# A Conformer stage in a two-layer trunk: block taps loaded by DMA, a fourth channel tile convolved on VectorE with its sum in PSUM, 24 low halves of weights made on GpSimd

## The chip, the cores and the metric

The kernel runs on one core of one Trainium2 chip. A core has a matrix engine (TensorE, "PE" in the profile; its weight loads are "PEld"), a vector engine (VectorE, "DVE"), a scalar engine (ScalarE, "ACT"), a general engine (GpSimd, "POOL"), and a queue that issues transfers between the chip's memory and the core (SyncE, "SP"). Each engine works through its own list of instructions in order and waits on semaphores for the others. SBUF is the core's working memory of 128 partitions, and PSUM a smaller one of eight banks, each 128 partitions x 512 float32, in which TensorE leaves its results.

The metric is the device time of one execution in microseconds. Lower is better.

## The reference

The program is a decoder trunk of two layers over 512 positions of 1024 channels, float32 throughout. Layer 0 mixes positions by a gated DeltaNet, layer 1 by a Conformer convolution; each layer then attends to a memory of 256 rows and applies an MLP of width 4096. The change lies in layer 1's Conformer:

```python
def conformer_conv(h, w_pw1, b_pw1, w_dw, b_dw, ln_g, ln_b, w_pw2, b_pw2):
    u = h @ w_pw1 + b_pw1
    u = u[..., :D_MODEL] * jax.nn.sigmoid(u[..., D_MODEL:])
    c = causal_depthwise_conv(u, w_dw) + b_dw
    c = jax.nn.silu(layer_norm(c, ln_g, ln_b))
    return c @ w_pw2 + b_pw2
...
for layer in range(DEPTH):
    if layer % 2 == 0:
        h = h + gated_deltanet(rms_norm(h, dn_norm[j]), ...)
    else:
        h = h + conformer_conv(rms_norm(h, cv_norm[j]), ...)
    h = h + memory_cross_attention(rms_norm(h, xa_norm[layer]), rms_norm(mem, ...), ...)
    h = h + sq_relu_mlp(rms_norm(h, mlp_norm[layer]), ...)
return rms_norm(h, final_norm)
```

The depthwise convolution is causal and has 31 taps per channel. `w_pw1` maps 1024 channels to 2 x 1024 (a value and a gate), `w_pw2` 1024 to 1024.

## The kernel before

**Products.** Every float32 product is made of three matrix products of halves. A weight block of 128 x 1024 comes in as `raw` (line 203); ACT casts it to the high half `wh` (line 214), and DVE subtracts that from `raw` to give the low half `wl` (line 215; the profile shows line 72, the helper `tt`). The activations are split likewise. `mm3` then adds high x high, high x low and low x high (lines 230 to 232). A block with its two halves is called a unit here; it gives 24 matmuls. Units are taken in a fixed order, the list `order`. `wnext` loads raw blocks some units ahead (`NRAW` = 3 buffers) and splits them ahead (`NW` = 3 buffers for each half). A raw buffer can be loaded again when both halves of the block that it held are made.

**The Conformer stage.** Activations are held as channels on partitions and positions along them, in eight channel tiles of 128 x 512; position t stands at column (t mod 4, t div 4), so that four phases lie beside each other. The stage goes through `CONV_SEQ`: 16 pw1 units (two for each channel tile m: value and gate), then 16 units of layer 1's K and V, which belong to the cross-attention that follows and depend on the memory alone. They keep TensorE supplied while the convolution is finished.

When both pw1 units of a tile are done, `pw_ev` scales them by the norm (`sg` and `pa`, DVE reading PSUM), applies the sigmoid on ACT, and multiplies. A tile is then convolved in one of two ways:

- Tiles 0 to `NDVE` - 1 = 2 go by taps on VectorE (`dve_conv`). The product is written into a padded copy `x7` with three more shifted phases. The first tap is an ACT multiplication into `ca`; 30 `scalar_tensor_tensor` instructions on DVE (line 75, `ca<-x,prm,ca`) then each add one tap: x times a scalar plus the sum, 128 x 512. They are kept in a list `todo`, from which `taps_dve` takes some after each unit, at `TAP_RATE` per microsecond. `turn` transposes the sum by four TensorE transposes (`cvT`, line 1041) and adds it into Y.
- Tiles 3 to 7 go by block form on TensorE (`conv`). Sixteen transfers copy `glu` into `xg` (line 1014), with 32 channels x 4 phases on the partitions. For each group j of 32 channels, nine matmuls (lines 1057 and 1060) multiply `xg` with block tap matrices, so 36 matmuls for a tile. The block taps, nine tiles of 128 x 512 for each channel tile, are made by `taps`: POOL multiplies a broadcast identity with a broadcast row of `prm`.

Both ways end in Y, which holds positions on partitions and channels along them and starts as the bias `b_dw`; for each quarter of the positions, DVE adds into `cy` and takes statistics `bn`. When all eight tiles are there, `ln` normalizes Y, and `ln_out` transposes it back (`lnT`), applies scale, bias and silu on ACT and splits the result for pw2.

**What sets the order.** `CONV_AFTER` says after which unit of `CONV_SEQ` each of these is issued: ("t", m) block taps, ("c", m, ...) groups of a block convolution, ("d", m) the transposes of a DVE tile, ("l", 0) the LayerNorm, ("o", m) `lnT`. The block taps of tile 3 are made in layer 0's MLP. A list scheduler then orders the instructions of each engine by its own estimate of when they are due; it may put instructions of one engine in another order than the program's. SP's queue carries the weights and the `xg` copies in such an order too.

**Memory.** `slot` hands out SBUF buffers of 128 x 512 from a pool of `NSLOT` = 66, `psum` banks from a pool of eight. A request waits until the oldest holder is done.

Of the kernel before, what the change touches and what calls it, by code (L numbers as in the profile page):

```python
# [8 lines left out]
F32 = mybir.dt.float32  # L9
F32R = mybir.dt.float32r  # L10
AF = mybir.ActivationFunctionType
ALU = mybir.AluOpType
AX = mybir.AxisListType

P = 128
NT = 512
NDVE = 3
KT = 8
EPS = 1e-6
LN_EPS = 1e-5  # L20
# [3 lines left out]
OFF = {n: 8 * i for i, n in enumerate(_VECS)}  # L24
_o = 8 * len(_VECS)
# [1 line left out]
_o += 16  # L27
OFF["w_conv"] = _o
_o += 24 * 4
OFF["w_dw"] = _o  # L30
_o += 8 * 144
OFF["w_tap"] = _o
_o += NDVE * 31
OFF["out_norm"] = _o
# [3 lines left out]


@with_exitstack  # L40
def tile_trunk(ctx, tc, xT, memT, prm_d, adt_d, bdw_d, fin_d, w_ab, w_kq, w_v, w_z, w_dno, w_pw1, w_pw2,
               w_q, w_k, w_vv, w_o, w_up, w_dn, yT):
    nc = tc.nc
    pe, act, dve, pool = nc.tensor, nc.scalar, nc.vector, nc.gpsimd
# [14 lines left out]
    def slot(dt=F32, s="u", shape=(P, NT)):  # L59
        return up.tile(list(shape), dt, tag="u", name=nm(s))  # L60
# [7 lines left out]
    def const(shape, s, dt=F32):  # L68
        return cp.tile(list(shape), dt, tag=s, name=s)

    def tt(e, o, a, b, op):
        e.tensor_tensor(out=o, in0=a, in1=b, op=op)  # L72

    def stt(o, a, s, b, op0, op1):
        dve.scalar_tensor_tensor(out=o, in0=a, scalar=s, in1=b, op0=op0, op1=op1)  # L75
# [7 lines left out]
    def c4(t):  # L83
        return t.rearrange("p (c i) -> p c i", c=4)
# [4 lines left out]
    def over_c(t, n=4):  # L89
        return t.unsqueeze(1).to_broadcast([P, n, t.shape[1]])  # L90


    prm = const([P, NPRM], "prm")
# [9 lines left out]
        return r  # L103

    nc.sync.dma_start(out=prm[:, 0:NVEC], in_=prm_d[:, 0:NVEC])
    wab = const([P, P], "wab")
    nc.sync.dma_start(out=wab, in_=w_ab)
    raw0 = wp.tile([P, 1024], F32, tag="raw", name="raw0", bufs=NRAW)
    nc.sync.dma_start(out=raw0, in_=w_kq[0][:, 0:1024])
# [4 lines left out]
    ident = const([P, P], "ident")  # L114
# [21 lines left out]
    headx = const([P, 32], "headx")  # L136
    dve.tensor_reduce(out=headx, in_=ident.rearrange("p (x c) -> p x c", c=4), op=ALU.add, axis=AX.X)
    dve.tensor_reduce(out=headm, in_=headx.rearrange("p (a h) -> p h a", h=8), op=ALU.add, axis=AX.X)
    ident4 = const([P, 32], "ident4")
    eps_rms = const([P, 1], "eps_rms")  # L140
    pool.memset(eps_rms, EPS)
    eps_ln = const([P, 1], "eps_ln")
# [3 lines left out]
    order, srcs = [], {}  # L146
# [26 lines left out]
    for kind, gq in DN_ORDER:  # L173
        for i in range(2):
            j = gq * 2 + i
# [30 lines left out]
    def wsplit():  # L206
        u = ws["split"]
        ws["split"] += 1
        while ws["load"] <= u:
            wload()  # L210
        raw = ws["raw"].pop(u)
        h = wp.tile([P, 1024], F32R, tag="wh", name=nm("wh"), bufs=NW)
        lo = wp.tile([P, 1024], F32R, tag="wl", name=nm("wl"), bufs=NW)
        act.copy(h, raw)  # L214
        tt(dve, lo, raw, h.bitcast(F32), ALU.subtract)
        ws["hl"][u] = (h, lo)

    def wnext(key, hf):
# [544 lines left out]
    def mem_gain(layer, half):  # L763
        gn = f"xa_mem{layer}"
        if half == 0:
            mem["xs"] = []
        for j in (2 * half, 2 * half + 1):
            mh = slot(F32R, "mh")
            ml = slot(F32R, "ml")
            for i in range(2):  # L770
                ks = slice(i * 256, (i + 1) * 256)
                src = mem["n"][j][:, ks]
                g = pc(gn, 2 * j + i)
                act.activation(mh[:, ks], src, AF.Copy, scale=g)
                stt(ml[:, ks], src, g, mh[:, ks].bitcast(F32), ALU.mult, ALU.subtract)
                mem["xs"].append((mh[:, ks], ml[:, ks]))

    KV = {}
# [191 lines left out]

    def taps(m):

        w = OFF["w_dw"] + 144 * m
        TAPS[m] = []
        for i in range(9):
            t = slot(s="tap")
            tt(pool, t.rearrange("p (a c) -> p a c", c=32), over_c(ident4, 16),
               prm[:, w + 16 * i:w + 16 * i + 16].unsqueeze(2).to_broadcast([P, 16, 32]), ALU.mult)
            TAPS[m].append(t)

    def conformer(norm, hres, nxt):
        xs = norm.xs
        st, xg = {}, {}
# [35 lines left out]

        def dve_conv(m, x7):  # L1020

            a = acc[m] = slot(s="ca")

            def tap(d):
                w, u, e = pc("w_tap", m * 31 + 30 - d), d // 4, d % 4
                src = x7[:, 3 - e:7 - e, 8 - u:136 - u]
                if d == 0:
                    act.activation(c4(a), src, AF.Copy, scale=w)
                else:
                    stt(c4(a), src, w, c4(a), ALU.mult, ALU.add)  # L1030

            return [lambda d=d: tap(d) for d in range(31)]

# [91 lines left out]

    nc.sync.dma_start(out=prm[:, NVEC:NPRM], in_=prm_d[:, NVEC:NPRM])
    nc.sync.dma_start(out=adt, in_=adt_d.partition_broadcast(P))
    for b in range(4):
        bs = slice(32 * b, 32 * b + 32)
        pool.tensor_copy(ident4[bs, :], ident[bs, bs])  # L1130
    abp = const([P, 2 * P], "abp", F32R)
    ab3 = abp.rearrange("p (k x) -> p k x", k=KT)
    act.copy(ab3[:, :, 0:16], wab.rearrange("p (k x) -> p k x", k=KT))
    tt(dve, ab3[:, :, 16:32], wab.rearrange("p (k x) -> p k x", k=KT), ab3[:, :, 0:16].bitcast(F32), ALU.subtract)
# [129 lines left out]
    n2 = Norm("mlp_norm0")  # L1264
    h = xattn(0, n1, h, n2)
    n3 = Norm("cv_norm", deng=pool)
    h = mlp(0, n2, h, n3, lambda: (mem_gain(1, 0), mem_gain(1, 1), taps(3)))
    n4 = Norm("xa_norm1")
    h = conformer(n3, h, n4)
    n5 = Norm("mlp_norm1")  # L1270
# [12 lines left out]
    def finish(hid, cur):  # L1283
# [3 lines left out]
        for c, g in LAST:  # L1287
# [14 lines left out]
            if g == 0:  # L1302
# [14 lines left out]
    mlp(1, n5, h, None, None, finish, load)  # L1317


NSLOT = 66  # L1320
NCV = 6
NRAW = 3
PRE = ((2, 4), (2, 6))
# [17 lines left out]
REC = (39, 68)  # L1341
MEM = 53
MLP_ORDER = [("up", 0), ("up", 1), ("dn", 0), ("up", 2), ("dn", 1), ("up", 3), ("dn", 2), ("dn", 3)]
TAP_RATE = 0.75
CONV_SEQ = [("p", i) for i in range(16)] + [("k", i) for i in range(16)]
CONV_AFTER = [(3, ("t", 4)), (9, ("c", 3, 0, 1)), (11, ("c", 3, 2, 3)), (11, ("t", 5)), (12, ("c", 4, 0, 1)),
              (13, ("c", 4, 2, 3)), (13, ("t", 6)), (14, ("c", 5, 0, 1, 2, 3)), (14, ("t", 7)), (15, ("d", 0)),
              (16, ("c", 6, 0, 1, 2, 3)), (17, ("d", 1)), (18, ("c", 7, 0, 1, 2, 3)), (20, ("d", 2)), (20, ("l", 0))]
CONV_AFTER += [(24 + _m, ("o", _m)) for _m in range(8)]


# [18 lines left out]

def _taps(np, w):

    wt = w.T.reshape(8, 4, 32, 31)
    e = np.zeros((4, 32, 8, 4, 9, 4), w.dtype)
    for s in range(4):
        for u in range(9):
            for r in range(4):
                d = r - s + 4 * u
                if 0 <= d <= 30:
                    e[s, :, :, :, u, r] = wt[:, :, :, 30 - d].transpose(2, 0, 1)  # L1380
    e = e.reshape(128, 8, 4, 9, 4)
    return np.concatenate([e[:, :, :, 0:8].reshape(128, 8, 128), e[:, :, :, 8].reshape(128, 8, 16)],
                          axis=2).reshape(128, 1152)


def _layout(np, i):
    i = {k: np.asarray(v) for k, v in i.items()}
    f = np.ascontiguousarray

    def vec(v):  # L1390
        return v.reshape(-1, 128).T

    r = {}
    r["xT"] = f(i["x"][0].T)
    r["memT"] = f(i["mem"][0].T.reshape(4, 2, 128, 256).transpose(0, 2, 1, 3).reshape(4, 128, 512))
    vecs = [i["dn_norm"][0], i["cv_norm"][0], i["xa_norm"][0], i["xa_norm"][1], i["xa_mem_norm"][0],
            i["xa_mem_norm"][1], i["mlp_norm"][0], i["mlp_norm"][1], i["cv_ln_g"][0],
            i["cv_ln_b"][0], i["cv_b_pw2"][0], i["cv_b_pw1"][0]]
    cols = [vec(v) for v in vecs]
    cols.append(i["dn_w_conv"][0].T.reshape(24, 128, 4).transpose(1, 0, 2).reshape(128, 96))  # L1400
    cols.append(_taps(np, i["cv_w_dw"][0]))
    cols.append(i["cv_w_dw"][0].T.reshape(8, 128, 31)[:NDVE].transpose(1, 0, 2).reshape(128, NDVE * 31))
    cols.append(i["dn_out_norm"][0].reshape(128, 1))
    r["prm"] = f(np.concatenate(cols, axis=1))
    r["adt"] = f(np.concatenate([i["dn_a_log"][0], i["dn_dt_bias"][0]]))
    r["bdw"] = f(i["cv_b_dw"][0])
    r["fin"] = f(i["final_norm"])
    w = i["dn_w_in"][0]
    r["w_ab"] = f(w[:, 4096:].reshape(8, 128, 16).transpose(1, 0, 2).reshape(128, 128))
    r["w_kq"] = _pack_a(np, w[:, :2048], [8, 9, 10, 11, 0, 1, 2, 3, 12, 13, 14, 15, 4, 5, 6, 7])  # L1410
    r["w_v"] = _pack_a(np, w[:, 2048:3072])
    r["w_z"] = _pack_b(np, w[:, 3072:4096])
    r["w_dno"] = _pack_a(np, i["dn_w_out"][0])
    r["w_pw1"] = _pack_a(np, i["cv_w_pw1"][0], [m for h in range(8) for m in (h, 8 + h)])
    r["w_pw2"] = _pack_a(np, i["cv_w_pw2"][0])
    r["w_q"] = np.stack([_pack_a(np, i["xa_w_q"][j]) for j in range(2)])
    r["w_k"] = np.stack([_pack_a(np, i["xa_w_kv"][j][:, :1024]) for j in range(2)])
    r["w_vv"] = np.stack([_pack_b(np, i["xa_w_kv"][j][:, 1024:]) for j in range(2)])
    r["w_o"] = np.stack([_pack_a(np, i["xa_w_o"][j]) for j in range(2)])
    r["w_up"] = np.stack([_pack_a(np, i["mlp_w_up"][j]) for j in range(2)])  # L1420
    r["w_dn"] = np.stack([np.concatenate([(_pack_b if (j, g) == (1, 3) else _pack_a)(
        np, i["mlp_w_down"][j][g * 1024:(g + 1) * 1024]) for g in range(4)]) for j in range(2)])
    return r
# [17 lines left out]
```

## Time and profile before

| | |
|---|---|
| median of 3 runs | 1583.6 us |
| lowest and highest | 1582.46 and 1584.26 us |
| the profiled execution, whole | 1584.79 us |
| its span in the profile | 1583.1 us |
| TensorE clock granted in it (1 is full) | 0.984 |

The span runs from the first to the last instruction that the profiler recorded; the whole time of the same execution is 1.7 us longer. The page cuts the span in 40 slices of about 39.6 us and gives the busy share of each engine in tenths:

```profile
PE   8997997999999999999999999999999999999998
DVE  6785787576555444343445599974545443443441
ACT  6655574645444433231424321164434432322332
POOL 1225224402111100000021316102012000000000
PEclk9998998799999999999999999999999999999999
```

The Conformer stage lies at about 880 to 1096 us, slices 23 to 28 counted from 1. A row of a timeline has a start, a length, the engine, the line, the operation, the tiles (output, then inputs) and a count where several stand together; idle time before it and what ended it follow in brackets. A row of groups has the count, then busy time in all and the mean of one in nanoseconds, then idle time of the engine before them. A row of waits has the time in all, how often, and the longest. A row of windows has the stretch and its length, then for each engine the busy time and the count, the clock granted, the share of time in which the transfer engines were busy, and the rate in GB/s. Instructions of one engine overlap by some 0.08 us, so lengths add up to a little more than the time that passes.

### The profile page before, as it was taken

The numbers are of one execution on the slowest core, as the hardware profiler recorded it, in microseconds if no ns is written. First come the engines' busy times: TensorE is split into PE (matmuls) and PEld (weight loads), VectorE is DVE, ScalarE is ACT, GpSimd is POOL, SyncE is SP. The second block draws the span as 40 slices with busy tenths as digits, with TensorE's granted clock in tenths as the row PEclk, the third lists the DMA queues.
The fourth block names the chain that finished last, engine by engine and source line by source line (L and its number), as shares of the span: only waits on it lengthen the run. The fifth ranks groups of instructions, "written<-read, shape, count | busy, mean of one in ns | idle before, by whom it ended". The sixth has DMA issues, their size and how long they took to land.

```text
span 1583.1 us, 19556 instructions
## 1 busy us (share of the span) xinstructions
PE 1539.9 (97%) x7690; PEld 1300.1 (82%) x7690; DVE 897.3 (57%) x1290; ACT 652.5 (41%) x997; POOL 239.5 (15%) x287
## 2 busy tenths in 40 slices
PE   8997997999999999999999999999999999999998
PEld 6886885898888888888888889888888888888886
DVE  6785787576555444343445599974545443443441
ACT  6655574645444433231424321164434432322332
POOL 1225224402111100000021316102012000000000
PEclk9998998799999999999999999999999999999999
DMA  5221112153211233223223422253212232223231
GB/s 180 67 80 54 59 49 94 54 173 119 91 61 64 93 98 102 94 94 101 98 94 95 146 79 92 77 164 103 80 41 94 93 104 96 94 96 104 94 107 53
DMA packets 46699, 147.57 MB, mean 93 GB/s; under 512 B 6288, under 2 KB 8976, under 8 KB 46608
## 3 DMA queue, kind: packets, MB, share of 16 engines
q1 hardware_dynamic: 46608, 146.33, 28.4%
q8 instruction: 60, 0.98, 0.3%
q14 instruction: 31, 0.25, 0.0%
HBM read 142.90 MB, written 2.10 MB: 92 GB/s over the span
## 4 chain that ended last, share of the span: by engine, by line
PE 79%; DVE 11%; ACT 4%; issue 2%; POOL 2%; SPq 1%; DMA 1%; DVEq 0%; POOLq 0%; ACTq 0%
PE up L230 7%; PE up L232 7%; PE up L231 7%; PE dn L232 6%; PE dn L231 6%; PE dn L230 6%; DVE ca L75 3%; PE q L230 2%; PE xo L231 2%; DVE wl L72 2%; PE q L231 2%; PE q L232 2%; PE xo L232 2%; PE xo L230 2%; PE pw L230 2%
## 5 line engine op out<-in xcount | busy, mean ns | idle before, releaser
L214 ACT CAST wh<-raw 128x1024 fp32r<-128x1024 f32 x248 | 260.2, 1051 | 699.6 <-PE dn L231 190.4
L72 DVE TENSOR_TENSOR wl<-raw,wh 128x1024 fp32r<-128x1024 f32 x248 | 310.3, 1252 | 128.6 <-ACT wh L214 122.5
L230 PE MATMUL up<-xh,wh 128*128 128x512 f32 x512 | 200.2, 391 | 0.0
L232 PE MATMUL up<-xh,wl 128*128 128x512 f32 x512 | 199.2, 389 | 0.0
L231 PE MATMUL up<-xl,wh 128*128 128x512 f32 x512 | 199.2, 389 | 0.0
L232 PE MATMUL dn<-uh,wl 128*128 128x512 f32 x448 | 174.3, 389 | 0.0
L230 PE MATMUL dn<-uh,wh 128*128 128x512 f32 x448 | 174.3, 389 | 0.0
L231 PE MATMUL dn<-ul,wh 128*128 128x512 f32 x448 | 174.3, 389 | 0.0
L72 DVE TENSOR_TENSOR h<-dn,h 128x512 f32<-128x512 f32 x56 | 41.8, 747 | 165.3 <-PE dn L232 165.3
L75 DVE SCALAR_TENSOR_TENSOR rl<-up,rb 128x512 f32<-128x512 f32 x64 | 44.2, 691 | 157.0 <-PE up L232 157.0
L231 PEld LDWEIGHTS up<-xl,wh 128*128 128x128 f32 x512 | 96.1, 188 | 20.4 <-issue 0.5
L230 PEld LDWEIGHTS up<-xh,wh 128*128 128x128 f32 x512 | 96.1, 188 | 20.2 <-issue 0.5
L232 PEld LDWEIGHTS up<-xh,wl 128*128 128x128 f32 x512 | 96.1, 188 | 20.0
L72 POOL TENSOR_TENSOR tap<-ident,prm 128x512 f32<-128x512 f32 x45 | 59.4, 1351 | 332.5 <-PE up L232 263.8
L231 PEld LDWEIGHTS dn<-ul,wh 128*128 128x128 f32 x448 | 84.1, 188 | 17.5
L230 PEld LDWEIGHTS dn<-uh,wh 128*128 128x128 f32 x448 | 84.1, 188 | 17.5
L232 PEld LDWEIGHTS dn<-uh,wl 128*128 128x128 f32 x448 | 84.1, 188 | 17.4
L72 POOL TENSOR_TENSOR sq<-sq,sq 128x512 f32<-128x512 f32 x30 | 49.9, 1663 | 252.7 <-ACT sq L305 167.8
L75 DVE SCALAR_TENSOR_TENSOR ca<-x,prm,ca 128x512 f32<-128x512 f32 x90 | 81.9, 911 | 2.1
L230 PE MATMUL h<-xh,wh 128*128 128x512 f32 x192 | 77.0, 401 | 1.4 <-ACT xh L298 1.4
L231 PE MATMUL h<-xl,wh 128*128 128x512 f32 x192 | 76.3, 397 | 1.5 <-DVE xl L75 1.5
L232 PE MATMUL h<-xh,wl 128*128 128x512 f32 x192 | 75.3, 392 | 0.0
(330 smaller groups left out, 3074.9 us busy)
## 6 DMA issues: line engine op xcount, KB each, us to landing
raw<-w_up SPq DMA_DIRECT2D x64, 512.0 KB, 3.4
raw<-w_dn SPq DMA_DIRECT2D x64, 512.0 KB, 3.5
raw<-w_pw SPq DMA_DIRECT2D x24, 512.0 KB, 3.6
raw<-w_kq SPq DMA_DIRECT2D x16, 512.0 KB, 3.6
raw<-w_k SPq DMA_DIRECT2D x16, 512.0 KB, 3.6
raw<-w_vv SPq DMA_DIRECT2D x16, 512.0 KB, 3.7
raw<-w_q SPq DMA_DIRECT2D x16, 512.0 KB, 3.4
raw<-w_o SPq DMA_DIRECT2D x16, 512.0 KB, 3.5
```

What stands on the lines that cost most here:

```text
L72: e.tensor_tensor(out=o, in0=a, in1=b, op=op)
L75: dve.scalar_tensor_tensor(out=o, in0=a, scalar=s, in1=b, op0=op0, op1=op1)
L214: act.copy(h, raw)
L230: pe.matmul(ps, wh, xh, start=first, stop=False)
L231: pe.matmul(ps, wh, xl, start=False, stop=False)
L232: pe.matmul(ps, wl, xh, start=False, stop=last)
```

## The change

Three things change in the Conformer stage.

1. *Block taps.* The host builds the block tap matrices in full, and `taps` loads them: nine transfers of 128 x 512 float32 (256 KB) for each of four tiles, on SP's queue. The small identity `ident4` and the 1152 columns of `prm` that held the compact taps are gone.
2. *A fourth tile on VectorE.* `NDVE` is 4: tile 3 is convolved by 31 taps. For all four tiles the running sum `ca` lies in a PSUM bank; after the last tap ACT copies it to an SBUF slot, from which the transposes read. `TAP_RATE` rises to 1.1, and `CONV_AFTER` is set anew: no block convolution of tile 3, and a fourth ("d", m).
3. *Low halves on GpSimd.* `wsplit` makes the low half on POOL for all 16 pw1 units and for the first half of each of layer 1's eight K and V blocks: 24 units. The other units stay on DVE.

Two constants used at the start, `wab` and `abp`, become slots, and `NSLOT` rises to 69.

```diff
-NDVE = 3
+NDVE = 4
...
-    wab = const([P, P], "wab")
+    wab = slot(s="wab")[:, 0:P]
...
     def wsplit():
...
         act.copy(h, raw)
-        tt(dve, lo, raw, h.bitcast(F32), ALU.subtract)
+        (kind, i, *j), hf = order[u]
+        gp = kind == "pw1" or j and kind in "KV" and i == 1 and hf == 0
+        tt(pool if gp else dve, lo, raw, h.bitcast(F32), ALU.subtract)
...
     def taps(m):
 
-        w = OFF["w_dw"] + 144 * m
         TAPS[m] = []
         for i in range(9):
             t = slot(s="tap")
-            tt(pool, t.rearrange("p (a c) -> p a c", c=32), over_c(ident4, 16),
-               prm[:, w + 16 * i:w + 16 * i + 16].unsqueeze(2).to_broadcast([P, 16, 32]), ALU.mult)
+            nc.sync.dma_start(out=t, in_=tap_d[m - NDVE, i])
             TAPS[m].append(t)
...
         def dve_conv(m, x7):
 
-            a = acc[m] = slot(s="ca")
-
             def tap(d):
                 w, u, e = pc("w_tap", m * 31 + 30 - d), d // 4, d % 4
                 src = x7[:, 3 - e:7 - e, 8 - u:136 - u]
                 if d == 0:
-                    act.activation(c4(a), src, AF.Copy, scale=w)
-                else:
-                    stt(c4(a), src, w, c4(a), ALU.mult, ALU.add)
+                    st["ca"] = psum("ca")
+                    act.activation(c4(st["ca"]), src, AF.Copy, scale=w)
+                    return
+                a = c4(st["ca"])
+                stt(a, src, w, a, ALU.mult, ALU.add)
+                if d == 30:
+                    acc[m] = slot(s="ca")
+                    act.copy(acc[m], st.pop("ca"))
...
-    for b in range(4):
-        bs = slice(32 * b, 32 * b + 32)
-        pool.tensor_copy(ident4[bs, :], ident[bs, bs])
-    abp = const([P, 2 * P], "abp", F32R)
+    abp = slot(F32R, "abp")[:, 0:2 * P]
...
-    h = mlp(0, n2, h, n3, lambda: (mem_gain(1, 0), mem_gain(1, 1), taps(3)))
+    h = mlp(0, n2, h, n3, lambda: (mem_gain(1, 0), mem_gain(1, 1), taps(NDVE)))
...
-NSLOT = 66
+NSLOT = 69
...
-TAP_RATE = 0.75
+TAP_RATE = 1.1
...
-CONV_AFTER = [(3, ("t", 4)), (9, ("c", 3, 0, 1)), (11, ("c", 3, 2, 3)), (11, ("t", 5)), (12, ("c", 4, 0, 1)),
-              (13, ("c", 4, 2, 3)), (13, ("t", 6)), (14, ("c", 5, 0, 1, 2, 3)), (14, ("t", 7)), (15, ("d", 0)),
-              (16, ("c", 6, 0, 1, 2, 3)), (17, ("d", 1)), (18, ("c", 7, 0, 1, 2, 3)), (20, ("d", 2)), (20, ("l", 0))]
+CONV_AFTER = [(3, ("t", 5)), (11, ("d", 0)), (12, ("c", 4, 0, 1)), (13, ("c", 4, 2, 3)), (13, ("t", 6)),
+              (14, ("c", 5, 0, 1, 2, 3)), (14, ("t", 7)), (15, ("d", 1)), (16, ("c", 6, 0, 1, 2, 3)), (18, ("d", 2)),
+              (18, ("c", 7, 0, 1, 2, 3)), (21, ("d", 3)), (21, ("l", 0))]
...
 def _taps(np, w):
...
+    t = np.zeros((8 - NDVE, 9, 4, 32, 16, 32), w.dtype)
+    for c in range(32):
+        t[:, :, :, c, :, c] = e[:, c].transpose(1, 2, 0, 3)
+    return t.reshape(8 - NDVE, 9, 128, 512)
```

More of the change, by code (lines that the diff above doesn't have):

```diff
@@ L29 @@
 _o += 24 * 4
-OFF["w_dw"] = _o
-_o += 8 * 144
 OFF["w_tap"] = _o
@@ L40, in tile_trunk @@
 @with_exitstack
-def tile_trunk(ctx, tc, xT, memT, prm_d, adt_d, bdw_d, fin_d, w_ab, w_kq, w_v, w_z, w_dno, w_pw1, w_pw2,
+def tile_trunk(ctx, tc, xT, memT, prm_d, adt_d, bdw_d, tap_d, fin_d, w_ab, w_kq, w_v, w_z, w_dno, w_pw1, w_pw2,
                w_q, w_k, w_vv, w_o, w_up, w_dn, yT):
@@ L138, in tile_trunk @@
     dve.tensor_reduce(out=headm, in_=headx.rearrange("p (a h) -> p h a", h=8), op=ALU.add, axis=AX.X)
-    ident4 = const([P, 32], "ident4")
     eps_rms = const([P, 1], "eps_rms")
@@ L1381, in _taps @@
     e = e.reshape(128, 8, 4, 9, 4)
-    return np.concatenate([e[:, :, :, 0:8].reshape(128, 8, 128), e[:, :, :, 8].reshape(128, 8, 16)],
-                          axis=2).reshape(128, 1152)
+    e = np.concatenate([e[:, :, :, 0:8].reshape(128, 8, 128), e[:, :, :, 8].reshape(128, 8, 16)], axis=2)
+    e = e.reshape(4, 32, 8, 9, 16)[:, :, NDVE:]
+    t = np.zeros((8 - NDVE, 9, 4, 32, 16, 32), w.dtype)
+    for c in range(32):
+        t[:, :, :, c, :, c] = e[:, c].transpose(1, 2, 0, 3)
+    return t.reshape(8 - NDVE, 9, 128, 512)
 def _layout(np, i):
@@ L1400, in _layout @@
     cols.append(i["dn_w_conv"][0].T.reshape(24, 128, 4).transpose(1, 0, 2).reshape(128, 96))
-    cols.append(_taps(np, i["cv_w_dw"][0]))
     cols.append(i["cv_w_dw"][0].T.reshape(8, 128, 31)[:NDVE].transpose(1, 0, 2).reshape(128, NDVE * 31))
@@ L1406, in _layout @@
     r["bdw"] = f(i["cv_b_dw"][0])
+    r["tap"] = f(_taps(np, i["cv_w_dw"][0]))
     r["fin"] = f(i["final_norm"])
```

## The prediction

> **What bounds the kernel now.** I read the page first: the busy shares, then the chain of waits.
>
> ```profile
> span 1583.1 us, 19556 instructions
> PE 1539.9 (97%) x7690; PEld 1300.1 (82%) x7690; DVE 897.3 (57%) x1290; ACT 652.5 (41%) x997; POOL 239.5 (15%) x287
> PE 79%; DVE 11%; ACT 4%; issue 2%; POOL 2%; SPq 1%; DMA 1%; DVEq 0%; POOLq 0%; ACTq 0%
> ```
>
> TensorE is busy for all but 43.2 us (1583.1 - 1539.9), so time can fall only by taking work from it or by closing its gaps. DVE's 57% is a mean, and the change acts in one stage; so next the busy time of each engine in the Conformer, cut where its phases change (pw1 from 898; the block convolutions mixed with pw1, then with the K units; V with lnT).
>
> ```profile
> 898.00:934.00 36.00, 36.00 (x161) 29.80 (x160) 33.74 (x47) 11.47 (x15) 0.00 (x0) 1.00 0.25 78
> 934.00:998.00 64.00, 64.00 (x423) 58.16 (x422) 62.87 (x74) 10.72 (x12) 37.73 (x27) 1.00 0.29 89
> 998.00:1037.00 39.00, 35.25 (x290) 35.05 (x290) 37.96 (x91) 10.66 (x13) 0.00 (x0) 0.96 0.28 88
> 1037.00:1064.00 27.00, 25.53 (x128) 20.89 (x127) 20.13 (x25) 20.56 (x27) 0.00 (x0) 1.00 0.54 176
> ```
>
> The columns after the length are PE, PEld, DVE, ACT and POOL. Up to 1037 PE and DVE are both full: 135.25 and 134.57 of 139 us. The waits of the stage name what ends PE's idle time:
>
> ```profile
> PE K L232 <- DVE wl L72: 3.7, 1, 3.7
> PE V L262 <- DVE wl L72: 1.5, 1, 1.5
> ```
>
> Both gaps, 5.2 us, end with a low half of a weight that stood behind other work on DVE. Work may therefore leave PE only as far as DVE follows.
>
> **The change part by part.** *TensorE.* Tile 3 now costs two pairs of block-form convolutions between pw units; a tile on the DVE path costs four transposes.
>
> ```profile
> 934.16 1.95 PE L1057 MATMUL cv<-tap,xg 128*128 128x128 f32 x16
> ...
> 938.10 0.48 PE L230 MATMUL pw<-xh,wh 128*128 128x512 f32 x1
> ...
> 949.07 1.95 PE L1057 MATMUL cv<-tap,xg 128*128 128x128 f32 x16
> ...
> 953.01 0.47 PE L230 MATMUL pw<-xh,wh 128*128 128x512 f32 x1
> ...
> 991.07 0.60 PE L1041 MATMUL cvT<-ident,ca 128*128 128x128 f32 x4
> 991.42 0.36 PE L230 MATMUL K<-mh,wh 128*128 128x256 f32 x1
> ...
> 994.37 1.95 PE L1057 MATMUL cv<-tap,xg 128*128 128x128 f32 x16
> ...
> 1037.45 0.93 PE L1088 MATMUL lnT<-ident,cy 128*128 128x128 f32 x7
> ...
> 1064.20 0.48 PE L230 MATMUL pw<-lsh,wh 128*128 128x512 f32 x1
> ```
>
> Start to start, 3.94 + 3.94 = 7.88 us go and 991.42 - 991.07 = 0.35 come: PE has 7.5 us less. With the 5.2 us of gaps closed as well, 12.7 is the most that this stage can give. The same rows give the lengths for the walk below: two pw units from 938.10 to 949.07, 5.5 each; a K unit 994.37 - 991.42 = 2.95; a whole block convolution, twice 3.94, 7.9; a V unit with its lnT (1064.20 - 1037.45 - 1.5) / 8 = 3.2.
>
> *The price of a tap.* 30 taps are added to 90, and all 120 move their sum to PSUM.
>
> ```profile
> L75 DVE SCALAR_TENSOR_TENSOR ca<-x,prm,ca 128x512 f32<-128x512 f32 x90 | 81.9, 911 | 2.1
> ...
> 902.32 0.74 DVE L75 SCALAR_TENSOR_TENSOR ca<-x,prm,ca 128x512 f32<-128x512 f32 x1
> 902.98 0.68 DVE L72 TENSOR_TENSOR pa<-pw,rb 128x512 f32<-128x512 f32 x1
> ...
> 909.28 3.89 DVE L75 SCALAR_TENSOR_TENSOR ca<-x,prm,ca 128x512 f32<-128x512 f32 x5
> ...
> 886.91 10.11 POOL L72 TENSOR_TENSOR tap<-ident,prm 128x512 f32<-128x512 f32 x9
> ...
> 967.71 11.22 DVE L75 SCALAR_TENSOR_TENSOR ca<-x,prm,ca 128x512 f32<-128x512 f32 x10
> ...
> 969.14 6.87 POOL L72 TENSOR_TENSOR tap<-ident,prm 128x512 f32<-128x512 f32 x5 [5.40 <-PE cv L1057]
> ```
>
> Operations overlap, so what counts is the pitch. A tap followed by another operation holds DVE for 902.98 - 902.32 = 0.66 us; five taps on one sum, each needing the last, took 3.89, or 0.78 (0.787 with the 0.74 of the last one taken off over four steps). While POOL made block taps, ten took 11.22: 1.12 each, and POOL's own went from 1.12 (10.11 / 9) to 1.37 (6.87 / 5). They slow each other. In the order of the changed build 51 of the 120 taps stand right behind one on the same sum and 69 have something between: without contention the mean is (51 x 0.787 + 69 x 0.66) / 120 = 0.714. Today's mean is 0.911 less the overlap of 0.08, or 0.83.
>
> Does a sum in PSUM escape the contention? What DVE did while POOL multiplied:
>
> ```profile
> 951.61 4.96 POOL L72 TENSOR_TENSOR tap<-ident,prm 128x512 f32<-128x512 f32 x4 [7.91 <-DMA xg<-glu]
> ...
> 954.58 0.68 DVE L72 TENSOR_TENSOR sg<-pw,rb 128x512 f32<-128x512 f32 x1
> ...
> 955.77 1.34 DVE L75 SCALAR_TENSOR_TENSOR ca<-x,prm,ca 128x512 f32<-128x512 f32 x1
> ```
>
> The operation with one operand in PSUM (pw) kept its 0.68; the tap, both operands in SBUF, took 1.34. So I take escape as likely, and it matters, for POOL stays busy with low halves. [...]
>
> No row shows DVE writing PSUM, let alone adding into it. Nearest rows:
>
> ```profile
> L75 DVE SCALAR_TENSOR_TENSOR h<-pw,prm,h 128x512 f32<-128x512 f32 x8 | 6.0, 751 | 20.9 <-PE pw L232 20.9
> L72 DVE TENSOR_TENSOR sg<-pw,rb 128x512 f32<-128x512 f32 x8 | 5.5, 683 | 1.5 <-PE pw L232 1.5
> L72 DVE TENSOR_TENSOR lsl<-la,lsh 128x512 fp32r<-128x512 f32 x8 | 5.5, 692 | 1.3 <-ACT lsh L267 1.1
> ```
>
> Reading PSUM is not dearer: 683 against 692 from SBUF, and 751 for the form of a tap against 0.74-0.75. I bound a tap in PSUM from 0.66 (dependence hidden) to 0.911 (a whole tap's mean today, nothing overlapped), and take 0.714, being nearest to the reading rows. [...]
>
> *Low halves on GpSimd.* 24 move. On DVE:
>
> ```profile
> L72 DVE TENSOR_TENSOR wl<-raw,wh 128x1024 fp32r<-128x1024 f32 x248 | 310.3, 1252 | 128.6 <-ACT wh L214 122.5
> L72 POOL TENSOR_TENSOR sq<-sq,sq 128x512 f32<-128x512 f32 x30 | 49.9, 1663 | 252.7 <-ACT sq L305 167.8
> 885.92 1.04 POOL L72 TENSOR_TENSOR dg<-ident,rstd 128x512 f32<-128x512 f32 x1 [9.20 <-DVE rstd L320]
> ```
>
> POOL's two-input operations of half the width take 1.04 to 1.66, so a low half takes 2.1 to 3.3; I take 2.5, twice the 1.12-1.37 of a tap. A pw unit of 5.5 us needs one, made up to NW = 3 units ahead: hidden, even at 3.3. Of the K and V units every second one is POOL's, so it has one per 5.9 us (K) or 6.4 (V with lnT). The cover is PE's own length; without it each would cost at most its 3.3. Of the 19 low halves that DVE makes from 898 to 1037 (one per unit, counted in the timeline), 15 leave it: 15 x (1.25 - 0.08) = 17.5 us.
>
> *Block taps by DMA.* POOL's 45 multiplications go. 36 transfers of 256 KB enter SP's queue, behind that tile's sixteen xg transfers:
>
> ```profile
> 957.81 10.02 SPq L1014 DMA_DIRECT2D xg<-glu  x16
> ```
>
> ```profile
> raw<-w_pw SPq DMA_DIRECT2D x24, 512.0 KB, 3.6
> ```
>
> Nine issues at no more than xg's 10.02 / 16 = 0.63 us are 5.6; the last lands at best 3.6 later (half the bytes of a raw transfer, so no more), 9.2 in all, and at worst at the rate of one raw transfer, 2.36 MB x 3.6 / 0.512 = 16.6. I take 9.2, as transfers overlap. Tiles 4 and 5 are far ahead. Tile 6's glu ends on DVE at about 966, so its xg issues run to 976.3, its taps land at 985.5, and its convolution stands on PE at 987 (walk below): 1.5 us to spare. Before tile 7's taps stands the raw transfer of a late K unit, which now waits for a low half on POOL (987); behind it queue these taps, landing by 997 for a convolution at 1003, and the weights after them, which are three units ahead.
>
> *The rest at nothing:* the first nine tap multiplications, under MLP matmuls; the second parameter transfer, shorter by 574 KB, which at that raw rate is 4 us if early weights wait behind it and 0 if not (0, since that transfer is issued beside eight others whose landing PE needs first); the ACT copy of each sum before its transposes, under a pw or K unit but for the last, which is in the walk (uncovered, 0.8 each); two constants that become slots.
>
> *The sum.* Twice. By load: DVE gains 30 x 0.714 = 21.4 and loses 17.5 and 90 x (0.83 - 0.714) = 10.4, net 6.5 less, against 7.5 less on PE. If DVE sets the end as now, the gain is about 6.5. By walking both queues: from 934.16 the new order on PE is two pw units, cvT, a pw unit, half of tile 4, pw, the other half, pw, tile 5, pw, cvT, a K unit: 987 for tile 6, which ends at 995. On DVE sg, pa and glu of tile 7 stand behind cy and bn of tile 6, which wait for that end; so glu comes at 998.3, its xg issues (10.02 to 11) run to 1008.7, and the last convolution, spread among K units, is stretched by about 1.0 us. After it DVE has seven taps (7 x 0.787 = 5.5), eight cy and bn (1.6 at 0.2) and a low half (1.2), then ACT copies (0.8) and signals pass (0.5): the last transposes come 9.6 after it, where PE, with its K units done, is ready at 7.3: 2.3 us. Stalls 3.3, gain 12.7 - 3.3 = 9.4. I take the middle, 8: 1584.8 - 8 = 1576.8 for a profiled execution of 1584.79. The runs' median, 1583.6, lies 1.2 below that: **1575.6**.
>
> **The rivals.** *A, all stalls go:* the scheduled order fits and taps run at 0.66; 1583.6 - 12.7 = 1571. Against it the late glu of tile 7.
> *B, VectorE becomes the bound, slower:* adding into PSUM is dearer when the next tap needs the sum. Every 0.01 us on a tap is 1.2 us; at 0.787 for all, 120 x 0.073 = 8.8 and the gain is gone. That is the turning point; at 0.85 the loss is 16.3, or 1592; at 0.911, 1599. For it: no row of writing PSUM, and dependent pitches already above 0.66. Against it: 683 against 692.
> *C, the contention stays:* POOL has some 20 low halves, 50 us, inside the taps' stretch. 27 multiplications of 37.73 us cost the taps 10.4; in proportion 13.8, so 1575.6 + 13.8 = 1589. Against it the 0.68 beside 1.34.
> *D, SP's queue:* block taps land after 16.6 us instead of 9.2; tile 6 is 6 us late; 1581.6, no change. For it: 1.5 us to spare. Against it: the mean DMA share of that stage, 0.29 in its row.
>
> **How the numbers follow.** Forecast 0.54 (1572.5 to 1580), A 0.13, B 0.18, C 0.06, D 0.09. A measurement of this kernel tells 0.2%, or 3.2 us, from no change. Faster: 0.54 + 0.13 = 0.67; same: D and the 0.02 of B near its turning point, 0.11; slower 0.16 + 0.06 = 0.22. The range takes in A and the mild ends of B and C, 1570.5 to 1589.
>
> **What would show it.** Right: ca near 0.75 single and unchanged under wl on POOL; wl there near 2.5; pw2 starting 7 to 10 us before its 1064.2; two gaps of 1 and 2 us before cv of tile 7 and the last cvT. Wrong: dependent taps pitched above 0.787 or ca above 0.9 beside POOL; PE waiting for cv's taps (D) or for POOL's wl; any change outside 880 to 1064, which the sum leaves at nothing.

## The result, and the profile after

| kernel | median (runs) | ratio to before, 95% interval | first pw | pw2 begins |
|---|---|---|---|---|
| before | 1583.48 us (17) | 1 | 877.92 | 1064.20 |
| changed | 1580.12 us (17) | 0.9978 [0.9971, 0.9986] | 880.84 | 1060.73 |

The change is 3.4 us faster, where 8 were forecast: the right sign, inside the range, less than half of the size. The profiled execution's span fell by the same 3.4, so its trace can say where the rest is. The last two columns are start times on TensorE, in the two profiled executions, and cut the difference in two. First the rows of the kernel before, from TensorE's timeline, then those of the changed kernel:

```profile
877.92 0.39 PE L230 MATMUL pw<-xh,wh 128*128 128x512 f32 x1
```

```profile
span 1579.7 us, 19402 instructions
```

```profile
880.84 0.39 PE L229 MATMUL pw<-xh,wh 128*128 128x512 f32 x1
...
1060.73 0.48 PE L229 MATMUL pw<-lsh,wh 128*128 128x512 f32 x1
```

The Conformer's first pw begins 2.92 us **later** than before, and pw2 3.47 earlier. So the stage gained 6.39 us, and 2.92 were lost ahead of it, in layer 0, where the forecast had put nothing. What follows pw2 is equal (518.9 us before, 519.0 now).

The stage itself, from first pw to pw2, as one window of each kernel (length; then busy time and count of PE, PEld, DVE, ACT, POOL; clock granted; share and rate of transfers). Before, then changed:

```profile
877.92:1064.20 186.28, 181.07 (x1088) 160.51 (x1086) 162.68 (x241) 60.88 (x76) 48.83 (x37) 0.99 0.35 110
```

```profile
880.84:1060.73 179.89, 175.42 (x1019) 153.93 (x1018) 145.21 (x249) 64.64 (x82) 53.91 (x24) 0.98 0.47 153
```

TensorE's busy time fell by 5.65 us and its idle time from 5.21 to 4.47. VectorE's busy time fell by 17.5, to 145 of 180 us: it is no longer full, before the LayerNorm either (118.4 of the 129 us from 898 to 1027, where the kernel before has 124.6). Yet TensorE waits for it nearly as long as before, at two new places. The waits of TensorE in the stage of the changed kernel (total, times, longest):

```profile
PE cvT L1041 <- ACT ca L1030: 2.3, 1, 2.3
PE lnT L1088 <- DVE cy L79: 1.9, 2, 1.5
PE cv L1057 <- DMA xg<-glu: 0.2, 1, 0.2
```

And the waits cost more than their own time. Windows around them:

```profile
880.84:1021.50 140.66, 140.33 (x839) 124.09 (x837) 117.96 (x207) 38.55 (x48) 44.18 (x20) 1.00 0.47 157
1021.50:1031.40 9.90, 7.61 (x53) 7.62 (x54) 6.68 (x19) 5.13 (x7) 2.35 (x1) 0.83 0.40 132
1031.40:1037.00 5.60, 3.75 (x19) 2.66 (x18) 5.56 (x9) 3.86 (x4) 2.59 (x1) 1.00 0.45 119
1037.00:1041.60 4.60, 4.60 (x17) 3.71 (x17) 2.66 (x4) 1.59 (x3) 0.00 (x0) 0.63 0.52 182
1041.60:1060.73 19.13, 19.13 (x98) 15.85 (x97) 12.35 (x13) 15.52 (x22) 4.79 (x2) 1.00 0.46 143
```

Behind the wait of 2.3 us the granted clock is 0.83 on the mean of ten microseconds, behind those of 1.9 us it is 0.63. Single matmuls show it: the K matmuls behind the last cvT, then those of V behind the lnT, take 0.41 and 0.63 us where 0.28 and 0.39 are usual.

```profile
1023.79 1.12 PE L1041 MATMUL cvT<-ident,ca 128*128 128x128 f32 x4 [2.31 <-ACT ca L1030]
...
1026.20 0.41 PE L230 MATMUL K<-ml,wh 128*128 128x256 f32 x1
...
1026.95 0.28 PE L231 MATMUL K<-mh,wl 128*128 128x256 f32 x1
...
1037.98 0.63 PE L260 MATMUL V<-wh,mh 128*128 128x512 f32 x1
...
1040.51 0.39 PE L260 MATMUL V<-wh,mh 128*128 128x512 f32 x1
```

The prices of the new operations came out as forecast. Groups of the changed kernel (busy in all, mean ns):

```profile
L73 DVE SCALAR_TENSOR_TENSOR ca<-x,prm,ca 128x512 f32<-128x512 f32 x120 | 88.0, 750 | 3.0 <-ACT ca L1024 1.2
L70 POOL TENSOR_TENSOR wl<-raw,wh 128x1024 fp32r<-128x1024 f32 x24 | 57.6, 2404 | 117.6 <-ACT wh L211 117.6
```

A tap is 0.750 us instead of 0.911, a low half on GpSimd 2.40 (2.5 forecast). What happened at the start shows on ScalarE. Before, then changed:

```profile
7.58 5.01 ACT L298 ACTIVATE xh<-x,prm 128x512 fp32r<-128x512 f32 x8
12.49 4.26 ACT L305 ACTIVATE sq<-x 128x512 f32<-128x512 f32 x8
16.66 1.99 ACT L214 CAST wh<-raw 128x1024 fp32r<-128x1024 f32 x2
```

```profile
8.06 4.39 ACT L297 ACTIVATE xh<-x,prm 128x512 fp32r<-128x512 f32 x7
15.27 1.05 ACT L211 CAST wh<-raw 128x1024 fp32r<-128x1024 f32 x1 [2.81 <-DMA raw<-w_kq]
16.22 0.72 ACT L297 ACTIVATE xh<-x,prm 128x512 fp32r<-128x512 f32 x1
16.84 1.04 ACT L211 CAST wh<-raw 128x1024 fp32r<-128x1024 f32 x1
17.78 4.27 ACT L304 ACTIVATE sq<-x 128x512 f32<-128x512 f32 x8
```

The high half of the second weight now stands ahead of the last scaled input and waits 2.81 us for its transfer; a third weight follows, and the squares that the first norm needs begin 5.3 us later. The sum of squares on TensorE (ssq) begins at 25.74 instead of 21.68. The scheduler put them so; the program's text for these instructions is the same.

### The profile page after: what moved, and what is told of

The parts are those of the page before. It is cut to its first block, busy times and chain, and to the rows that moved or that the text cites. A ratio compares the mean times of both kernels' runs of the same rounds, so it can differ in the third digit from the quotient of the medians.

```text
span 1579.7 us, 19402 instructions
## 1 busy us (share of the span) xinstructions
PE 1535.3 (97%) x7622; PEld 1293.8 (82%) x7622; DVE 879.1 (56%) x1296; ACT 655.7 (42%) x1003; POOL 237.1 (15%) x262
## 4 chain that ended last, share of the span: by engine, by line
PE 78%; DVE 10%; ACT 4%; issue 2%; POOL 2%; DMA 2%; SPq 1%; DVEq 0%; POOLq 0%; ACTq 0%
PE up L229 7%; PE up L231 7%; PE up L230 7%; PE dn L231 6%; PE dn L229 6%; PE dn L230 6%; DVE ca L73 3%; PE q L229 2%; PE xo L230 2%; PE q L231 2%; PE q L230 2%; PE xo L231 2%; PE xo L229 2%; PE pw L229 1%; PE pw L230 1%
## 5 line engine op out<-in xcount | busy, mean ns | idle before, releaser
L70 DVE TENSOR_TENSOR wl<-raw,wh 128x1024 fp32r<-128x1024 f32 x224 | 276.7, 1236 | 123.5 <-ACT wh L211 122.2
L230 PEld LDWEIGHTS dn<-ul,wh 128*128 128x128 f32 x448 | 84.1, 188 | 17.5
L73 DVE SCALAR_TENSOR_TENSOR ca<-x,prm,ca 128x512 f32<-128x512 f32 x120 | 88.0, 750 | 3.0 <-ACT ca L1024 1.2
L70 POOL TENSOR_TENSOR wl<-raw,wh 128x1024 fp32r<-128x1024 f32 x24 | 57.6, 2404 | 117.6 <-ACT wh L211 117.6
```

What stands on the lines that cost most here:

```text
L230: pe.matmul(ps, wh, xl, start=False, stop=False)
```

## The experiments

Each ratio is to the kernel before, run in the same job; 0.001 is 1.6 us. The intervals are 0.0017 to 0.0028 wide, 2.7 to 4.4 us, so differences of 2 us rest on the profiles and on repetition.

| run | median (runs) | ratio, 95% interval |
|---|---|---|
| after_again | 1578.30 (6) | 0.9967 [0.9955, 0.9978] |
| after_c | 1580.14 (11) | 0.9974 [0.9966, 0.9983] |
| f_front | 1575.53 (5) | 0.9953 [0.9941, 0.9966] |
| f_front2 | 1577.08 (6) | 0.9955 [0.9942, 0.9968] |
| f_const | 1576.21 (5) | 0.9955 [0.9942, 0.9967] |
| f_const2 | 1577.92 (5) | 0.9954 [0.9941, 0.9966] |
| f_pad | 1576.13 (5) | 0.9956 [0.9942, 0.9969] |
| b_slots | 1585.56 (11) | 1.0011 [1.0002, 1.0020] |
| b_short | 1583.62 (11) | 0.9993 [0.9984, 1.0002] |
| s_sbuf | 1601.85 (4) | 1.0114 [1.0100, 1.0128] |
| s_dvelow | 1588.94 (8) | 1.0030 [1.0020, 1.0041] |
| s_n3 | 1580.23 (11) | 0.9979 [0.9970, 0.9987] |
| b_dma | 1577.50 (6) | 0.9961 [0.9949, 0.9972] |
| t_d22o26 | 1571.52 (5) | 0.9923 [0.9911, 0.9936] |

### The start

Theory: the loss of 2.9 us comes from the new order at the start, which the two edits of layout there (the constants that became slots, the shorter parameter transfer) bring about. Rival: it is the spread of single executions, and the rest is missing in the stage. f_front takes both edits back:

```diff
-    wab = slot(s="wab")[:, 0:P]
+    wab = const([P, P], "wab")
...
-    abp = slot(F32R, "abp")[:, 0:2 * P]
+    abp = const([P, 2 * P], "abp", F32R)
...
+OFF["pad"] = _o
+_o += 1152
...
-NSLOT = 69
+NSLOT = 65
...
+    cols.append(np.zeros((128, 1152), np.float32))
```

> The changed kernel with its two small constants outside the slot pool again (65 slots) and with 1152 columns of zeros in the parameter table, so that the second parameter transfer has its old length. Every instruction from the MLP on stands as in the changed kernel, those of the first 300 us as in the kernel before. If the start lost the 2.9 us by which the Conformer began late (880.84 against 877.92), the time falls by 2.9 from the changed kernel, 1580.1 to 1577.2, a ratio of 0.996 to the kernel before; ssq begins near 21.7 us and the first pw near 878. If that offset was chance of one profile, the time stays at 1580.

> The changed kernel with the order of the kernel before at the start (constants outside the slots, the parameter transfer at its old length), again, now on the same chip as the control. In eleven profiles so far, first pw begins at 879.0 to 880.8 us with the short transfer and at 875.2 to 878.2 with the long one, 2.7 apart on the means. If that is the loss, the time is 2.7 below the control, 1576 to 1577; if the two fall within 1 us, the start is not what kept the change from its forecast.

> The changed kernel unaltered, as a control beside the others on one chip: 1580.1, ratio 0.998. If it comes out at 1576, the kernels with a mended start gained nothing over it, and the loss at the start is in doubt.

> The changed kernel unaltered, as the control on the same chip as the next: 1579 to 1580.

Measured: f_front2 is 3.1 us under its control after_c (1577.08 against 1580.14); f_front, in a job without a control, had 1575.53, and the other control 1578.30. ssq began at 20.7 and 20.9 us. First pw, though, began at 875.2 in the one and at 879.4 in the other profile: between ssq and there the two executions of this one kernel took 854.5 and 858.5 us, at a granted clock of 0.95 and 0.93 over the first 310 us, so one profile alone would not have settled it. Over all runs of this study, first pw begins at 879.0 to 880.8 where both edits stand (6 profiles, mean 880.0), and at 875.2 to 879.7 elsewhere (10 profiles, mean 877.5). The loss is confirmed, at 2 to 3 us: 3.1 by the pair in one job, 2.5 by the profiles, and 1.9 from the other control's ratio (0.9967) to f_front2's (0.9955).

Which edit is it? f_const takes back the constants alone (the four lines on `wab` and `abp` above, 68 slots), f_pad the transfer alone (66 slots); b_slots and b_short make the one and the other in the kernel before. In b_short the table of block taps comes in a transfer of its own, behind the first weights.

> The changed kernel with the two constants outside the slot pool (68 slots) and the short parameter transfer: the cast of abp stands first on ScalarE again, one high half still stands between the scaled inputs and their squares. If the place of that cast costs as much as the weights ahead of the squares, half of the 2.9 us comes back: about 1578.7. If the transfer's length alone counts, 1580.

> The changed kernel with the parameter transfer at its old length and the constants still slots (66 slots): the squares stand ahead of the second and third high halves again, the cast of abp stays late. If the order of the squares carries the loss, nearly all of it comes back: about 1577.7. If the place of abp carries it, 1580.

> The kernel before with the two constants as slots and nothing else: only the place of abp's cast and subtraction moves. If that place alone matters little, as the first matmul starts 0.5 us later in the changed kernel, 1584.0; if it carries the loss of the start, 1586.

> The kernel before with its block-tap table in a transfer of its own, issued after the first weights, so that the second parameter transfer is as short as in the changed kernel; nothing else. Up to the end of layer 0's attention the order on every compute engine is that of f_const. If the short transfer's order of ScalarE costs the start, ssq begins at 24 to 25 us, first pw near 880 and the time rises by about 2.4 to 1586; if the loss belongs to the constants that became slots, it stays at 1584.

> The changed kernel with its constants outside the slots and the short transfer, again. If the transfer's length carries the loss, 1579 to 1580 as the changed kernel; if the constants' place carries it, 1576 to 1577 as f_const's runs had it.

Measured: f_const and f_pad each win as much as both together (0.9954 to 0.9956). For f_pad that was the first of the two cases expected, for f_const neither. The granted clock does not make this difference: among executions with a mean clock of 0.982 to 0.984 the changed kernel (with its two controls) took 1581.0 us on the mean (11) and the five runs with a mended start, f_front to f_pad in the table, 1578.3 (9); among those at 0.986 to 0.988, 1579.1 (21) and 1575.7 (15). b_slots loses 1.7 us [0.3, 3.2], b_short nothing (1.1 faster, interval up to 0.3 slower). The costs do not add: each edit alone moves something at the start (abp's cast behind the first high half; or one high half ahead of the squares) and costs at most 1.7; only both together put a high half ahead of the last scaled input as well, and cost 2 to 3. That this one instruction carries the rest is argued from the order, not shown by a run of its own. A late ssq alone does not: it began at 24.0 us in f_const, 23.1 in f_const2 and 23.2 in b_short, later than the 21.7 of before, and none of them lost time. So which instruction carries the loss stays open.

### The parts of the change in the stage

s_sbuf puts the sums back in SBUF, s_dvelow takes the low halves back to VectorE, s_n3 takes tile 3 back to TensorE, each in the changed kernel.

```diff
-                    st["ca"] = psum("ca")
+                    st["ca"] = slot(s="ca")
...
-                    acc[m] = slot(s="ca")
-                    act.copy(acc[m], st.pop("ca"))
+                    acc[m] = st.pop("ca")
```

> The changed kernel with the running sum of the taps in an SBUF slot again, without the ACT copy at the end. If a sum in PSUM is what keeps the taps clear of the low halves on GpSimd, some 38 us of them (16 x 2.4) stand beside taps; 37.7 us of block-tap multiplications cost the taps 10.4 us in the kernel before, so taps rise from 0.70 to about 0.78 each on the mean, single ones beside GpSimd to 1.1 or more, low halves on GpSimd above 2.4, and with 8.9 us of idle time on VectorE to use up first some 3 to 8 us reach the end: 1583 to 1588. If the place of the sum does not matter, ca stays at 0.75 and the time at 1580.

```diff
-        tt(pool if gp else dve, lo, raw, h.bitcast(F32), ALU.subtract)
+        tt(dve, lo, raw, h.bitcast(F32), ALU.subtract)
```

> The changed kernel with all low halves on VectorE, the sums still in PSUM. VectorE takes back 15 low halves of 1.15 us before the LayerNorm, 17 us, against 8.9 us of idle time there: 8 to 12 us more, 1588 to 1592. If GpSimd's work hinders VectorE more than it takes off it, the time falls instead.

```diff
-NDVE = 4
+NDVE = 3
-TAP_RATE = 1.1
+TAP_RATE = 0.75
...
```

(`CONV_AFTER` is that of before here.)

> The changed kernel with tile 3 back in block form (NDVE 3, the old rate and places), and everything else of the change kept: block taps by DMA, sums in PSUM, low halves on GpSimd. TensorE gets 6.9 us back (7.70 of convolutions less 0.76 of transposes). If TensorE alone bounded the stage this gives 1587. If, as the trace of the changed kernel shows, its waits for VectorE (4.4 us) and the slow matmuls behind them (2.5 us) vanish with the fourth tile, the two cancel: about 1580, and the fourth tile brings next to nothing.

s_sbuf is 23.6 us above its control after_again (1601.85 against 1578.30), not 3 to 8: the direction held, the size did not. Its groups, then a tap on VectorE and what GpSimd did meanwhile:

```profile
L73 DVE SCALAR_TENSOR_TENSOR ca<-x,prm,ca 128x512 f32<-128x512 f32 x120 | 116.0, 978 | 2.8 <-ACT ca L1024 1.2
L70 POOL TENSOR_TENSOR wl<-raw,wh 128x1024 fp32r<-128x1024 f32 x24 | 63.3, 2640 | 133.7 <-ACT wh L211 112.4 <-DVE wl L70 21.3
```

```profile
904.40 0.74 DVE L73 SCALAR_TENSOR_TENSOR ca<-x,prm,ca 128x512 f32<-128x512 f32 x1
905.06 0.69 DVE L70 TENSOR_TENSOR pa<-pw,rb 128x512 f32<-128x512 f32 x1
905.66 2.29 DVE L73 SCALAR_TENSOR_TENSOR ca<-x,prm,ca 128x512 f32<-128x512 f32 x1
```

```profile
904.74 2.65 POOL L70 TENSOR_TENSOR wl<-raw,wh 128x1024 fp32r<-128x1024 f32 x1 [3.96 <-ACT wh L211]
```

While the low half runs (904.74 to 907.39), pa, with an operand in PSUM, takes its usual 0.69; the tap behind it, both operands in SBUF, ends only at 907.95, half a microsecond after GpSimd. So the tap stood until the other engine's instruction was over. That is no single case: 14 of the 120 taps took 2.75 us on the mean, the other 106 took 0.74, and each of the 14 ended 0.55 us after a low half on GpSimd. The kernel before shows the same with its shorter GpSimd instructions: 22 of its 90 taps took 1.41 on the mean, and each ended 0.55 us after a block-tap multiplication; in b_dma, where these are gone, all 90 took 0.73 to 0.75. Together the taps took 28 us more (116.0 - 88.0), and TensorE then waited 6.4 us for a sum and 11.3 for transfers (4.6 for `xg`, 6.7 for block taps). My estimate scaled the loss by GpSimd's busy time from block taps of 1.1 us each; what counts is how long one GpSimd instruction lasts, and how many taps one stops.

s_dvelow came as expected, 1588.94: VectorE makes 16 low halves from 898 to 1027 us instead of 4 and is busy for 121.7 of these 129 us, and TensorE waits 5.7 us for the sums and 5.2 for transfers. So the fourth tile needs the low halves on GpSimd here, and these need the sums in PSUM.

s_n3 came as expected too: 1580.23, 1.9 us above the control in its job where TensorE has 6.9 us more to do; its one wait on TensorE in the stage is 1.2 us. Its ratio, 0.9979 [0.9970, 0.9987], is that of the changed kernel's other runs (0.9978, 0.9974), so the fourth tile is worth 2 us at most, and a gain is not shown. That raised the question what the smallest part of the change does alone. b_dma is the kernel before with its block taps loaded by DMA; zeros keep the second parameter transfer at its old length, and the constants stay outside the slots, so that the start stands as before:

> The kernel before with its block taps loaded by DMA and nothing else changed: three tiles on VectorE, sums in SBUF, low halves on VectorE. GpSimd is idle beside the taps, so if contention made them dear they fall from 0.83 to about 0.71 each, 10 us of VectorE's time, and the two waits of 5.2 us and the slow matmuls behind them go: 1577. Then this part alone does what the whole change does. If the DMAs hold up the weights or the xg transfers on their queue, or the waits come from VectorE's order and not its load, it stays at 1583.

Measured 1577.50, as expected: 6.7 us under the kernel before in the same job, where the whole change (after_c) is 4.0 under it, and 7.1 with the start mended (f_front2). The stage of b_dma, first pw to pw2, and TensorE's one wait in it:

```profile
877.52:1057.38 179.86, 179.47 (x1087) 158.89 (x1086) 144.87 (x241) 61.54 (x76) 1.04 (x1) 1.00 0.51 166
```

```profile
PE cvT L1042 <- DVE ca L75: 0.4, 1, 0.4
```

179.86 us, against 179.89 of the changed kernel. TensorE is busy 179.47 here and 175.42 there: the fourth tile, the PSUM sums and the low halves on GpSimd take 4.05 us off it, and it idles 4.47 instead of 0.39, so 4.08 go to waits. A part of what was taken off comes back as well, in the slow matmuls behind these waits.

### The waits that are left

If those waits and the slow matmuls behind them are what was left, covering them must win 4 to 6 us more. t_d22o26 changes only where the end of the stage is issued, on top of f_front:

```diff
-              (18, ("c", 7, 0, 1, 2, 3)), (21, ("d", 3)), (21, ("l", 0))]
+              (18, ("c", 7, 0, 1, 2, 3)), (22, ("d", 3)), (22, ("l", 0))]
-CONV_AFTER += [(24 + _m, ("o", _m)) for _m in range(8)]
+CONV_AFTER += [(min(26 + _m, 31), ("o", _m)) for _m in range(8)]
```

> The kernel with the mended start, the last transposes and the LayerNorm issued one K unit later and the transposes back (lnT) two V units later, the last three together. TensorE then has 9.8 us of K units between the last block convolution and the last cvT, where VectorE needs 9.6, and 11 us before the first lnT, where it needs 10.5; before pw2 up to 0.7 us may be waited for. If the 4.2 us of waits in the stage, and the slow matmuls behind them, are what is left between the stage's gain and the most it can give, the time falls by 4 to 6 from f_front, to about 1571. If the waits only move to pw2, it stays at 1576.

Measured 1571.52, 0.9923, as expected: 5.6 us under f_front2 and 12.6 under the kernel before, both in the same job. Its stage, and its waits on TensorE:

```profile
876.97:1049.79 172.82, 172.09 (x1020) 151.48 (x1018) 141.31 (x246) 61.49 (x78) 54.32 (x24) 1.00 0.47 158
```

```profile
PE V L263 <- POOL wl L72: 0.4, 1, 0.4
PE cv L1059 <- DMA xg<-glu: 0.2, 1, 0.2
```

Idle time fell from 4.47 to 0.73 us against the changed kernel's profile, and busy time by 3.33 with the same matmuls, at a clock of 1.00: that is what the slow matmuls had cost in that execution. It is the fastest kernel of this study.

## Why the prediction was wrong

**The step that failed first** is "The rest at nothing", where it lists the second parameter transfer and "two constants that become slots". The transfer was priced by its bytes and the slots by their instructions, none. Both changed the order that the scheduler chose at the start, and together they cost 2 to 3 us: f_front and f_front2 win it back. The profiles put 2.9 of the 4.6 us that are missing from the 8 there; the other 1.6 are missing in the stage (6.39), where the forecast, the middle of two estimates, left out a wait of 1.85 us before the lnT and the slow matmuls behind waits. With the start mended the change gives 1575.5 and 1577.1 in two jobs, against the 1575.6 forecast. That agreement is partly luck: of the two estimates of the stage one was near for a wrong reason, and the other left out two terms of 3.5 us. Step by step:

- *TensorE's work.* 7.3 us less, for 7.5 forecast: start to start, the block convolutions went down by 7.70 and cvT up by 0.76, 0.4 of which is slow clock.
- *The price of taps and low halves.* 0.714 forecast as the mean pitch, 0.70 measured start to start; a run of nine on one sum took 7.09, or 0.79 each, the dependent pitch of before. Writing PSUM was not dearer (0.750 for a tap against 0.749, below); rival B fell. Low halves 2.40 for 2.5. But the mean pitch of before was not 0.83: overlap was taken off every tap, and 60 of the 90 did not overlap, the next tap on the same sum beginning 0.04 us after their end. Start to start, idle time taken off, the mean was 0.886, so 90 taps free VectorE of 15.5 us at the forecast pitch, not 10.4.
- *Escape from contention.* Right, and worth more than said: s_sbuf. Rival C fell. The trace of before holds more than "They slow each other": each of its 22 slow taps, 1.41 us on the mean, ended 0.55 us after a GpSimd instruction did, where an undisturbed tap takes 0.75. In s_sbuf, too, each of the 14 slow taps, 2.75 on the mean, ended 0.55 us after a low half on GpSimd: they waited out its instruction.
- *The place of the sum by itself.* 0.750 on the mean for a tap that reads and writes PSUM against 0.749 for the 68 undisturbed ones in SBUF of the kernel before: in this form of instruction it made no difference.
- *The transfers.* Tile 6's taps were issued from 980.04 and its convolution did not wait; rival D fell.
- *The walk.* Its glu of tile 7 ends at 1001.1, or 998.2 on the old start, where the walk had 998.3; the last cvT waited 2.31 us for 2.3 forecast; the last convolution 0.22 for 1.0. Its 0.8 for ACT's copy and 0.5 for signals were estimates that no row showed: the copy took 0.58, and from the last tap's end to the cvT 0.68 passed in all. The walk stopped there. It took for granted that the LayerNorm would be in time, and the lnT waited 1.85. Of the signs named, the two gaps were to come before cv of tile 7 and the last cvT; the first was next to nothing, and pw2 began 3.47 us earlier, not 7 to 10.
- *What a wait costs.* The walk counted idle time alone. The slow matmuls behind its waits cost another 3.3 us, and the kernel before had paid 1.6 behind its own (181.07 us of busy time, where b_dma does the same matmuls in 179.47): the windows from its first wait on (the wait itself lies in the first of them) show the clock at 0.87.

```profile
1005.00:1012.00 7.00, 3.25 (x21) 3.05 (x20) 6.95 (x16) 3.08 (x4) 0.00 (x0) 0.87 0.05 14
1012.00:1018.00 6.00, 6.00 (x49) 6.00 (x48) 5.82 (x15) 0.00 (x0) 0.00 (x0) 0.87 0.10 25
```

  So the most that the stage could give was not 12.7 but 14.2 (186.28 less the 172.09 of t_d22o26's busy time); t_d22o26 reached 13.5 of it (186.28 - 172.82).
- *The two estimates.* The load estimate, 6.5, is next to the stage's 6.39, but not for its reason: VectorE was not full. With 15.5 for 10.4 its net would have been 11.6 us less, more than PE's 7.5. It idled 8.9 us before the LayerNorm (3.2 of them for block convolutions to end, most of the rest for ScalarE), and the chain of late steps behind the last convolution set the time. The walk, 9.4, less the lnT's 1.85, plus the convolution's 0.8, less slow matmuls of 1.7 beyond those of before, gives 6.65, near the 6.39 measured.

## What to carry to other kernels

An edit that costs no work can still cost time where a scheduler decides the order: compare the order on every engine from the first instruction on, and ask of each instruction that moved what it waits for. A part that frees a full engine should be tried alone before work is moved to that engine; here loading the block taps gave the whole gain, and the other three parts paid only when the end of the stage was issued so that TensorE had work while the last tile was finished. A wait of TensorE is priced with the slow matmuls that it can bring: here a wait of some 2 us cost 1.4 to 2.0 more where they came.

## What was unexpected of the hardware

- Waits of 2.3 and 1.9 us on TensorE were followed by matmuls of 0.41 instead of 0.28 us and of 0.63 instead of 0.39, for 2 to 3 us each, but not every time. Eight profiles have these two waits at the same places: the clock fell to 0.83 in the ten microseconds around the first in four of them, and to 0.63 behind the second in seven. With both the stage took 179.9 us (three profiles), with one 178.4 to 178.6 (five). In these records the clock changes only on a grid of 3.41 us, and how the wait falls on that grid tells the cases apart. First two windows of the changed kernel's profile, then two of after_again, the same kernel with the same wait of 2.3 us (busy time of PE first, the clock granted third from the end):

```profile
1019.98:1023.40 3.42, 1.50 (x13) 1.29 (x11) 3.06 (x4) 1.29 (x2) 0.88 (x1) 1.00 0.82 213
1023.40:1026.81 3.41, 3.02 (x14) 3.03 (x15) 2.55 (x9) 1.31 (x3) 1.47 (x1) 0.50 0.44 163
```

```profile
1020.21:1023.62 3.41, 1.64 (x14) 1.65 (x15) 2.23 (x4) 1.98 (x4) 2.37 (x1) 1.00 0.51 165
1023.62:1027.04 3.42, 3.42 (x31) 3.42 (x30) 3.14 (x14) 1.56 (x2) 0.00 (x0) 1.00 0.43 153
```

  Over all 16 profiles, from 870 to 1090 us, each of the 20 windows of this grid at a clock of 1.00 that one at 0.50 follows had TensorE busy for at most 0.476 of its length, and each of the other 1001 at 1.00 for at least 0.483. No window lay between the two, and other kernels were not measured.
- A VectorE instruction with two SBUF operands beside a GpSimd instruction of 2.65 us took 2.29 instead of 0.74, while one with an operand in PSUM kept its 0.69. All 36 slow taps of the two kernels that have such pairs (s_sbuf 14, before 22) ended 0.55 us after a GpSimd instruction did.
